# Gate's and up's products by kind in three pairs, Strassen-like sums rewritten, and a residual one step behind its chunk, in a hybrid Fourier and SSD block on one core

## The chip, the cores and the metric

The kernel runs on 1 core of one Trainium2 chip. The metric is the device time of one execution in microseconds (us). Before the change the median of 3 runs is 2445.47 us (2444.1 to 2446.0).

## The reference

One layer of a flow-matching generator over 2048 latent tokens of width 1024, with 256 context tokens as a prefix, all in fp32. Cut to what the change touches:

```python
def swiglu(h, w_gate, w_up, w_down):
    return (jax.nn.silu(h @ w_gate) * (h @ w_up)) @ w_down
...
        hx = modulate(rms_norm(x, g_pre_mix[l]), sm_x, cm_x)
        u_f, z, xs, Bm, Cm, dt_raw = mixer_inputs(hx, ...)
        y, _, _ = ssd_bidir(xs, Bm, Cm, dt_raw, ...)
        x = x + gm_x * rms_norm(mixer_output(u_f, z, xs, y, d_skip[l], g_ssd[l], w_out[l]), g_post_mix[l])

        hx2 = modulate(rms_norm(x, g_pre_ffn[l]), sf_x, cf_x)
        x = x + gf_x * rms_norm(swiglu(hx2, w_gate[l], w_up[l], w_down[l]), g_post_ffn[l])
```

The mixer is a projection of the normed input, a Fourier part of 256 channels, a bidirectional chunked scan of 12 heads of 64 channels (chunks of 128 tokens), and an output projection to 1024. `w_gate` and `w_up` are 1024 x 2816, `w_down` is 2816 x 1024.

## The kernel before, in words

**Precision.** Every fp32 matrix is split into two halves: `hi`, its value rounded to the format fp32r, and `lo`, what is left. A product is hi·hi + hi·lo + lo·hi, three matmuls. ACT writes the hi half (a cast), and DVE or POOL the lo half (a subtraction).

**Chunk steps.** Once the projections are done, `chunk_step` runs for the chunks c = 15 to 1 and `last_step` for chunk 0. A step makes a chunk's scan outputs (`outputs_mm`, the state's part `off`, and `offb`, to which POOL's product `xq` is added), its gate, its norm, and its output projection into PSUM (`out_mm`), and beside these it prepares the next chunk: `scores`, `weights` (ACT shifts and exponentiates the decays `ab` in place), `state_terms`, `skip_terms`. Three names stand for chunks in flight: `ch` is this step's, `pv` the one before, `ppv` the one before that. `fourier_out` copies ch's Fourier outputs from PSUM into `ch.o`. In the next step `mix_out(pv)` adds the scan's part to `pv.o`, and ACT sums its squares. One more step later `mix_scale(ppv)` scales `ppv.o` by the norm (DVE, 128x1024) and `residual(ppv, G)` adds it on POOL to `ppv.xr`, the input's rows, and stores the sum as `x2`. Both `o` and `xr` are tiles of the tag `raw` with four buffers, which the weights' loads use as well; `xr` is loaded by `residual_load(pv)`. In eight of the steps `tile_norm` and `tile_modulate` read 128 rows of `x2` again, norm them, transpose them on PE and write them, modulated, into `xf`: two tiles (tag A) that hold the 1024 tokens of the first pass of the MLP, as feature blocks.

**Gate and up.** `gate_up(p, blocks, step, last)` runs for two passes p of 1024 tokens. Each pass has NJ = 11 pairs j of two 128-wide column blocks. For gate (m = 0) and up (m = 1) of a pair, the 2x2 block product is made by a scheme with seven products i = 0 to 6 instead of eight. One product is 12 matmuls of 128x512: a block of weights `wa` against a block `slot` of the tokens.
- Token blocks: `Blocks` makes seven blocks of 128x2048 from `xf`, some of them sums or differences of others (`sum`), and writes hi and lo halves (`parts`) into slots of the tags q, B and C. In the trace the tag's name is the tile's: `slot`, `actB`, `actC`; `actA` is xf, and `t2` a temporary sum.
- Weight blocks: quarters of a pair's weights are loaded into `raw` on the SP queue. `weight_block` returns one of them or a sum, `ws` (POOL, 128x512, three buffers); `make` casts it and subtracts (ACT, DVE), two halves in `wa`.
- Products go into PSUM banks (`mm`, and `mbank`), and their sums are gathered in `u2`, `u3` and `sg`; gate's sums go through SiLU on ACT, and are multiplied by up's on DVE or POOL. `hidden` makes four sums `hs` of the activations and stores them for the down projection.

`sequence(p, j)` sets the order of the 14 products: gate's seven, then up's seven. Only the first pair of pass 0 has an order of its own, which mixes the two. `stream` lists all of them, and `next_w` makes the weights ahead of their products in that order.

**What sets the order.** Instructions on an engine run in the order written, as the generators in `steps(...)` are advanced. The part from the first pair of pass 0 on is written out by hand: `steps(run, n)` lets `gate_up` issue n products, and between them stand the pieces of `xs0` (sums and parts), the last chunks' `mix_out`, `mix_scale` and `residual`. In the remaining pairs of pass 0 `beside` advances `prepare`, which norms, transposes and modulates the tokens of pass 1 into `xf1`, and in the last pair `last0(i)` writes block i of pass 1 once up's product i of pass 0 is issued. In the kernel of the trace all computing is recorded by one helper, so all rows carry its line, L140, and are told apart by their tiles.

Of the kernel before, what the change touches and what calls it, by code (L numbers as in the profile page):

```python
# [12 lines left out]
F32 = mybir.dt.float32  # L13
# [148 lines left out]
def fourier_ssd_block(ctx, tc, a):  # L162
# [625 lines left out]
    def quad_load(j, m, h):  # L788
        if (j, m, h) not in quads and j < 2 * NJ:
            c = 256 * (j % NJ)  # L790
            quads[j, m, h] = wload(GATE_UP[m][:, 4 * h : 4 * h + 4, c : c + 256], [P, 4, 256])

    def quad(j, m, r, h):
        quad_load(j, m, h)
        return quads[j, m, h][:, :, r * P : (r + 1) * P]

    def weight_block(j, m, i):
        a11, a21 = (quad(j, m, r, 0) for r in range(2))
        key = j, m
        if i == 0:  # L800
            return a11
        if i in (1, 3) and key not in sums:
            s1, s2 = (ta[0].tile([P, 4, P], F32, tag="ws", name="ws", bufs=3) for _ in range(2))
            G.tensor_tensor(s1, a21, quad(j, m, 1, 1), op=ALU.add)
            G.tensor_tensor(s2, s1, a11, op=ALU.subtract)
            sums[key] = s1, s2
        if i in (1, 3):
            return sums[key][i == 1]
        if i in (4, 5):
            return quad(j, m, i - 4, 1)  # L810
        s = ta[0].tile([P, 4, P], F32, tag="ws", name="ws", bufs=3)
        if i == 2:
            G.tensor_tensor(s, a11, a21, op=ALU.subtract)
        else:
            G.tensor_tensor(s, quad(j, m, 0, 1), sums.pop(key)[1], op=ALU.subtract)
        return s
# [3 lines left out]
    def make(kind, p, j, m, i):  # L820
# [53 lines left out]
    def down_parts(p, i, f):  # L874
# [7 lines left out]
        def temp():  # L882
            return ta[0].tile([P, 512], F32, tag="ws", name="wt", bufs=3)
# [252 lines left out]
    def residual_load(ch):  # L1136
        if ch.c > 1:
            ch.xr = wp.tile([P, D], F32, tag="raw", name="xr", bufs=4) if ch.c > 2 else g_.tile([P, D], F32, tag="acc", name="xr")
        dma(ch.xr, x_d[ch.c * P : (ch.c + 1) * P, :])
# [33 lines left out]
    normed = {}  # L1173
# [21 lines left out]
    def chunk_step(c, ch, nx, pv, ppv):  # L1195
# [26 lines left out]
        norms()  # L1222
        steps(st, 1)
        steps(w, 1)
        steps(st, 1)
# [15 lines left out]
        if pv:  # L1241
            residual_load(pv)
# [7 lines left out]
        steps(md)  # L1250
        if c in TILE_AT:
# [5 lines left out]
    def last_step(ch, pv, ppv):  # L1257
# [6 lines left out]
        mix_scale(ppv)  # L1264
        residual(ppv, V)
        quad_load(0, 0, 1)
# [3 lines left out]
        r1 = group_norm(ch)  # L1270
        feed_forward(ch, pv)
        steps(r1)
        steps(r2)
# [52 lines left out]
    with tc.manual_schedule(engines=ordered):  # L1326
# [229 lines left out]
        ch, pv, ppv = pend[0], None, None  # L1556
# [4 lines left out]
        def feed_forward(ch, pv):  # L1561
# [4 lines left out]
            ff.x = xs0 = Blocks(xf, ta[0], "xt")  # L1566
            xs0.place(0, 0)
# [5 lines left out]
            hs["gmix"], pv.xr, ch.xr, ch.o = (rows[:, i] for i in range(4))  # L1573
            dma(hs["gmix"], mods_d[0].rearrange("a d -> (a d)").partition_broadcast(P))
            residual_load(pv)
            residual_load(ch)
            fourier_out(ch)
            fetch(2)
# [4 lines left out]
        turn = [0]  # L1583

        def slot(i=None):

            tag = "qBCBqqC"[turn[0] % 7 if i is None else i]
            turn[0] += i is None
# [4 lines left out]
        def mbank(tag="m"):  # L1593
            return ff.pac.tile([P, 512], F32, tag=tag, name="m" + tag, bufs=3 if tag == "m" else 1)

        def parts_into(sl, src, engine=V):
            S.copy(sl[:, 0], src)
            engine.tensor_tensor(sl[:, 1], src, sl[:, 0].bitcast(F32), op=ALU.subtract)

        class Blocks:  # L1600


            def __init__(self, xf, pool, tag):
                self.xf, self.pool, self.tag, self.slots = xf, pool, tag, {}

            def place(self, i, fixed=None):
                self.slots[i] = slot(fixed)

            def sum(self, i):
                x1, x2 = self.xf  # L1610
                if i == 3:
                    V.tensor_tensor(x1[:, 0:4], x2[:, 0:4], x1[:, 0:4], op=ALU.subtract)
                elif i == 1:
                    self.t2 = [self.pool.tile([P, 2, 512], F32, tag=self.tag, name="t2") for _ in range(2)]
                    for h in range(2):
                        V.tensor_tensor(self.t2[h], x2[:, 4 + 2 * h : 6 + 2 * h], x1[:, 2 * h : 2 * h + 2], op=ALU.subtract)
                elif i == 2:
                    V.tensor_tensor(x2[:, 0:4], x2[:, 4:8], x2[:, 0:4], op=ALU.subtract)
                else:
                    for h in range(2):  # L1620
                        x = x1[:, 4 + 2 * h : 6 + 2 * h]
                        G.tensor_tensor(x, x, self.t2[h], op=ALU.subtract)

            def parts(self, i, engine=V):
                x1, x2 = self.xf
                sl = self.slots[i]
                if i == 1:
                    for h in range(2):
                        S.copy(sl[:, 0, 2 * h : 2 * h + 2], self.t2[h])
                        engine.tensor_tensor(sl[:, 1, 2 * h : 2 * h + 2], self.t2[h], sl[:, 0, 2 * h : 2 * h + 2].bitcast(F32),  # L1630
                                             op=ALU.subtract)
                else:
                    src = {0: x1[:, 0:4], 2: x2[:, 0:4], 3: x1[:, 0:4], 4: x1[:, 4:8], 5: x1[:, 4:8], 6: x2[:, 4:8]}[i]
                    parts_into(sl, src, engine)

        def gate_up(p, blocks, step, last):

            late = idle
            for j in range(NJ):
                apart = p == 0 and j == 0  # L1640
                if apart:
                    b1 = [mm()[:, 0, :], mbank("t")]
                else:
                    bb = mm()
                    b1 = [bb[:, m, :] for m in range(2)]
                sg = None
                st = [SimpleNamespace() for _ in range(2)]
                for m, i in sequence(p, j):
                    s = st[m]
                    if i in (1, 2, 3):  # L1650
                        s.b = getattr(s, "b", {})
                        s.b[i] = mbank()
# [11 lines left out]
                    elif i == 1:  # L1664
                        V.tensor_tensor(s.u2, s.u2, ps, op=ALU.add)
                    elif i == 2:
                        s.u3 = ta[0].tile([P, 512], F32, tag="u", name="u3", bufs=4)
                        V.tensor_tensor(s.u3, s.u2, ps, op=ALU.add)
# [291 lines left out]
```

## Time and profile before

| | |
|---|---|
| median of 3 runs | 2445.47 us (2444.1 to 2446.0) |
| the profiled execution | 2440.59 us, of which the trace's span is 2438.8 us |
| PE, matmuls | 2284.8 us busy, 94% of the span |
| PE, weight loads (beside the matmuls) | 1866.6 us, 77% |
| DVE | 1677.3 us, 69% |
| ACT | 1113.0 us, 46% |
| POOL | 1094.6 us, 45% |
| DMA | 377.20 MB, 155 GB/s on average |

The shares are averages over stages that differ: projections, scan, chunk steps, gate and up, down. A matmul counts as busy until its modelled end, also where it is stretched or its input is late. The chunk steps lie at 732 to 1084 us of the span, the first pairs of pass 0 at 1084 to 1220, and the change from pass 0 to pass 1 at 1525 to 1590.

### The profile page before, as it was taken

The page shows a single profiled execution, that of the slowest core. Times are in us where ns is not written, and L with a number is a line of the kernel's source. Part 1 is how long each engine was busy: PE and PEld are TensorE (multiplying, and loading weights), DVE is VectorE, ACT ScalarE, POOL GpSimd, SP SyncE. Part 2 cuts the span into 40 slices and gives each one's busy share as a digit, 9 for nine tenths or more (in the row PEclk, how much of TensorE's full clock was granted, in tenths as well). Part 3 has the DMA queues.
Part 4 walks back from the last instruction along what each step waited for, and adds up shares of the span by engine and source line. Part 5 has one row for each costly group of instructions (what it writes and reads, how often), then busy time and mean ns, then how long its engine had stood idle before and what let it go on. Part 6 is the DMA issues. An engine that isn't in the chain of part 4 may idle for free. (4 is left out here: it accounts for less than half of the span.)

```text
span 2438.8 us, 30217 instructions
## 1 busy us (share of the span) xinstructions
PE 2284.8 (94%) x10861; PEld 1866.6 (77%) x10861; DVE 1677.3 (69%) x2241; ACT 1113.0 (46%) x2019; POOL 1094.6 (45%) x681
## 2 busy tenths in 40 slices
PE   7999798899989999977999999799999999998998
PEld 3887667777778888765788888588888888877886
DVE  3569878698977777777555555855555575779666
ACT  4435453354338677765533333333333335444444
POOL 2122627545552444435546556546555451525512
PEclk9999998999999999998999999999999999999999
DMA  9355436355476887733333233243233364547333
GB/s 309 125 156 163 142 101 201 123 176 159 153 250 211 250 248 238 233 129 117 102 118 109 95 100 99 95 156 108 95 108 102 106 220 160 170 142 277 101 123 117
DMA packets 272580, 377.20 MB, mean 155 GB/s; under 512 B 17111, under 2 KB 190115, under 8 KB 269358
## 3 DMA queue, kind: packets, MB, share of 16 engines
q1 hardware_dynamic: 243062, 344.49, 44.6%
q10 hardware_dynamic: 29368, 30.78, 3.7%
q8 instruction: 86, 1.41, 0.2%
q14 instruction: 64, 0.52, 0.1%
HBM read 280.49 MB, written 94.72 MB: 154 GB/s over the span
## 5 line engine op out<-in xcount | busy, mean ns | idle before, releaser
L140 PE MATMUL b<-wd,hd 128*128 128x512 f32 x1848 | 426.6, 392 | 12.7 <-DVE hd L140 10.1
L140 PEld LDWEIGHTS b<-wd,hd 128*128 128x128 f32 x1848 | 348.5, 189 | 90.6 <-DVE hd L140 13.1
L140 PE MATMUL mm<-slot,wa 128*128 128x512 f32 x1560 | 374.9, 393 | 12.6 <-ACT u L140 5.3
L140 PEld LDWEIGHTS mm<-slot,wa 128*128 128x128 f32 x1560 | 293.9, 189 | 76.3 <-ACT u L140 5.7
L140 DVE SCALAR_TENSOR_TENSOR acc<-u,convw,acc 128x992 f32<-128x992 f32 (+5 forms) x228 | 310.6, 1366 | 23.5 <-ACT acc L140 19.1
L140 PE MATMUL mm<-actB,wa 128*128 128x512 f32 x1056 | 259.7, 394 | 12.6 <-DVE wa L140 5.6
L140 PE MATMUL mm<-actC,wa 128*128 128x512 f32 x1056 | 258.4, 394 | 10.1 <-DVE sg L140 5.1
L140 PEld LDWEIGHTS mm<-actB,wa 128*128 128x128 f32 x1056 | 200.1, 190 | 56.5 <-DVE wa L140 6.4
L140 PEld LDWEIGHTS mm<-actC,wa 128*128 128x128 f32 x1056 | 200.4, 190 | 53.4 <-DVE sg L140 5.5
L140 ACT CAST wa<-ws 128x512 fp32r<-128x512 f32 x176 | 109.1, 622 | 270.8 <-PE mm L140 253.3
L140 PE MATMUL mm<-actA,hi 128*128 128x512 f32 x704 | 227.7, 404 | 3.8 <-DVE actA L140 2.7
L140 POOL TENSOR_TENSOR rq_y<-rq_ms,mhalf 128x1 f32<-128x1 f32 (+2 forms) x60 | 52.8, 886 | 325.9 <-DVE rq_ms L140 316.3
L140 DVE TENSOR_TENSOR wa<-ws,wa 128x512 fp32r<-128x512 f32 x176 | 153.3, 872 | 49.4 <-ACT wa L140 47.6
L140 POOL TENSOR_TENSOR ws<-raw 128x512 f32<-128x512 f32 x88 | 121.4, 1379 | 125.4 <-DVE wa L140 120.9
L140 DVE TENSOR_TENSOR u<-u,mm 128x512 f32<-128x512 f32 x132 | 90.6, 686 | 123.3 <-PE mm L140 123.1
L140 DVE TENSOR_TENSOR wa<-raw,wa 128x512 fp32r<-128x512 f32 x132 | 127.4, 966 | 49.0 <-ACT wa L140 48.6
L140 PEld LDWEIGHTS mm<-actA,hi 128*128 128x128 f32 x704 | 130.2, 191 | 33.3 <-issue 4.1
L140 POOL TENSOR_TENSOR adacc<-adacc,adaw 128x1024 f32<-128x1024 f32 x28 | 74.0, 2641 | 182.0 <-ACT adaw L140 178.4
L140 ACT CAST wa<-raw 128x512 fp32r<-128x512 f32 x132 | 82.2, 623 | 152.2 <-PE mm L140 148.0
L140 POOL TENSOR_TENSOR lo<-raw,hi 128x1024 fp32r<-128x1024 f32 x34 | 90.2, 2654 | 127.5 <-ACT hi L140 127.5
L140 PE MATMUL mm<-actC,hi 128*128 128x512 f32 (+1 forms) x512 | 144.7, 370 | 0.0
L140 PE MATMUL mm<-actA,lo 128*128 128x512 f32 x352 | 139.3, 396 | 0.6 <-DVE lo L140 0.6
(286 smaller groups left out, 4452.3 us busy)
## 6 DMA issues: line engine op xcount, KB each, us to landing
hraw<-hg SPq DMA_DIRECT2D x70, 512.0 KB, 4.5
raw<-in_w_in_dram SPq DMA_DIRECT2D x54, 512.0 KB, 4.9
ab<-acsd SPq DMA_DIRECT2D x128, 192.0 KB, 4.3
raw<-in_w_gate_dram SPq DMA_DIRECT2D x44, 512.0 KB, 5.0
raw<-in_w_up_dram SPq DMA_DIRECT2D x44, 512.0 KB, 5.2
hg<-hs SPq DMA_DIRECT2D x22, 1024.0 KB, 5.0
adaw<-in_w_ada_dram SPq DMA_DIRECT2D x32, 512.0 KB, 3.8
l_x<-xtok SPq DMA_DIRECT2D x33, 384.0 KB, 6.1
```

The costliest lines, as they stand in the source:

```text
L140: r = issue(out, *args, **kw)
```

## The change

It has two parts that meet at the first pair of pass 0.

**In the chunk steps** `ppv` goes. `mix_scale` and `residual` now take `pv`, the chunk of the step before, and stand later in the step, behind the first parts of the next chunk's weights and states; `residual_load(ch)` loads this step's own `xr`; `fourier_out` moves down behind `norms()`. In four of the steps, and after four pieces of `prepare`, `third_sum` makes a 128x4x128 piece of one block difference (b22 - b12), which `Blocks` made as a whole before. `last_step` and `feed_forward` follow.

**In gate and up** three pairs, `TOGETHER` (the first and the last of pass 0, the first of pass 1), take the products by kind: gate's 0, up's 0, gate's 4, up's 4, then 2, 1, 3, 6 and 5. In them the banks of products 1 and 3 are `m2` for gate and `t` for up, one buffer each; every bank tag now has one buffer. The two multiplications by up's sums that POOL made go to DVE there. `Blocks` is rewritten: each of the sums is made in place on DVE right before its block's halves, and all lo halves are DVE's; the slot's tag is fixed by the block's number. The quarters of the weights are loaded in the order of their first use by a list, `quarters`, the next whenever the one four places back has had its last use. `ws` has four buffers.

```diff
+    TOGETHER = ((0, 0), (0, NJ - 1), (1, 0))
+
     def sequence(p, j):
-        if p == 0 and j == 0:
-            return [(0, 0), (1, 0), (0, 4), (0, 1), (0, 2), (0, 3), (0, 6), (1, 4), (0, 5), (1, 1), (1, 2), (1, 3), (1, 5), (1, 6)]
+        if (p, j) in TOGETHER:
+            return [(m, i) for i in (0, 4, 2, 1, 3, 6, 5) for m in range(2)]
         return [(m, i) for m in range(2) for i in range(7)]
...
-        if i == 3:
-            jn, mn = (j, 1) if m == 0 else (j + 1, 0)
-            for h in range(2):
-                quad_load(jn, mn, h)
+        while len(quads) < len(quarters) and last_use[quarters[len(quads) - 4]] <= pos[1]:
+            quad_load()
...
+    def third_sum(xf, t):
+
+        if t > 3:
+            x = xf[1][:, :, (7 - t) * P : (8 - t) * P]
+            V.tensor_tensor(x[:, 0:4], x[:, 4:8], x[:, 0:4], op=ALU.subtract)
...
         steps(r2)
-        if ppv:
-            mix_scale(ppv)
-            residual(ppv, G if nx else V)
+        if third:
+            third_sum(xf, third.pop())
         fourier_mm(ch)
         steps(wo_rest.pop() if wo_rest else idle)
-        fourier_out(ch)
         steps(w, 1)
         steps(st, 2)
         steps(sk, 1)
         norms()
+        fourier_out(ch)
         steps(st, 1)
         steps(w, 1)
+        if pv:
+            mix_scale(pv)
+            residual(pv, G)
         steps(st, 1)
...
-        if pv:
-            residual_load(pv)
+        residual_load(ch)
...
-            xs0.place(4, 4)
-            xs0.parts(4, G)
+            steps(r1)
+            xs0.parts(4)
...
+            quad_load()
             fetch(2)
-            xs0.sum(3)
-            xs0.sum(1)
...
-            def parts(self, i, engine=V):
-                x1, x2 = self.xf
-                sl = self.slots[i]
+                b11, b21, b12, b22 = x1[:, 0:4], x1[:, 4:8], x2[:, 0:4], x2[:, 4:8]
                 if i == 1:
...
+                    V.tensor_tensor(b11, b11, b12, op=ALU.add)
+                elif i == 3:
+                    V.tensor_tensor(b12, b22, b11, op=ALU.subtract)
+                elif i == 5:
+                    V.tensor_tensor(b21, b21, b11, op=ALU.subtract)
+                src = {0: b11, 1: b11, 2: b12, 3: b12, 4: b21, 5: b21, 6: b22}[i]
+                sl = self.slots[i] = slot(i)
+                S.copy(sl[:, 0], src)
+                V.tensor_tensor(sl[:, 1], src, sl[:, 0].bitcast(F32), op=ALU.subtract)
...
-                        s.b[i] = mbank()
+                        s.b[i] = mbank(({1: "m2", 2: "m0", 3: "m2"}, {1: "t", 2: "m1", 3: "t"})[m][i] if together else f"m{i - 1}")
...
-                                (G if i != 6 else V).tensor_tensor(out, out, c, op=ALU.mult)
+                                (V if together or i == 6 else G).tensor_tensor(out, out, c, op=ALU.mult)
...
         def last0(i):
-            if i == 0:
...
-                xs1.parts(i, G if i in (3, 5) else V)
+            xs1.parts(i)
```

How this moves instructions shows at three places.

ACT in one of the chunk steps, from the scores to the square of the step before: `ab<-ab,lda` are the shifts of the decays, `ab<-ab` the exponentials, `o<-mm` is `fourier_out`. Before:

```order
L140 COPY sc<-a 128x512
L140 ACTIVATE off<-yg 128x768
L140 COPY o<-mm 128x1024
L140 ACTIVATE ab<-ab,lda 128x128 x12
L140 ACTIVATE ab<-ab 128x384
L140 ACTIVATE ab<-ab,lda 128x128 x6
L140 ACTIVATE ab<-ab 128x384
L140 ACTIVATE ab<-ab,lda 128x128 x6
L140 ACTIVATE ab<-ab 128x384 x2
L140 CAST yh<-off 128x256
L140 ACTIVATE jk,sq_6287<-o 128x1024
```

and now:

```order
L140 COPY sc<-a 128x512
L140 ACTIVATE off<-yg 128x768
L140 ACTIVATE ab<-ab,lda 128x128 x6
L140 COPY o<-mm 128x1024
L140 ACTIVATE ab<-ab,lda 128x128 x6
L140 ACTIVATE ab<-ab 128x384
L140 ACTIVATE ab<-ab,lda 128x128 x6
L140 ACTIVATE ab<-ab 128x384
L140 ACTIVATE ab<-ab,lda 128x128 x6
L140 ACTIVATE ab<-ab 128x384 x2
L140 CAST yh<-off 128x256
L140 ACTIVATE jk,sq_6292<-o 128x1024
```

The first six shifts stand ahead of the copy of o now, the other six still behind it.

PE in the first pair of pass 0, one row for a product: the bank it goes to, the token block (`slot`, `actB`, `actC`) and the weights. Before:

```order
L140 MATMUL mm_9166<-slot_9114,wa_9117 128x512 x12
L140 MATMUL mt_9167<-slot_9114,wa_9128 128x512 x12
L140 MATMUL mm_9166<-slot_9120,wa_9168 128x512 x12
L140 MATMUL mm_9242<-actB_9232,wa_9175 128x512 x12
L140 MATMUL mm_9266<-actC_9233,wa_9195 128x512 x12
L140 MATMUL mm_9294<-actB_9234,wa_9212 128x512 x12
L140 MATMUL mt_9167<-slot_9120,wa_9267 128x512 x12
L140 MATMUL mm_9413<-actB_9232,wa_9327 128x512 x2
L140 MATMUL mm_9294<-actC_9235,wa_9245 128x512 x12
```

and now:

```order
L140 MATMUL mm_9171<-slot_9127,wa_9130 128x512 x12
L140 MATMUL mm_9171<-slot_9127,wa_9146 128x512 x12
L140 MATMUL mm_9171<-slot_9137,wa_9172 128x512 x12
L140 MATMUL mm_9171<-slot_9137,wa_9175 128x512 x12
L140 MATMUL mm0_9260<-actB_9192,wa_9197 128x512 x12
L140 MATMUL mm1_9286<-actB_9192,wa_9220 128x512 x12
L140 MATMUL mm2_9306<-actB_9215,wa_9242 128x512 x12
L140 MATMUL mt_9332<-actB_9215,wa_9265 128x512 x12
L140 MATMUL mm2_9355<-actC_9283,wa_9287 128x512 x12
L140 MATMUL mt_9381<-actC_9283,wa_9307 128x512 x12
L140 MATMUL mm2_9355<-actC_9325,wa_9334 128x512 x12
L140 MATMUL mt_9381<-actC_9325,wa_9357 128x512 x12
```

Each token block is used by two products that follow each other, gate's and up's, where before several blocks were used by one product and again many places later; the banks `mm2` and `mt` come back after two products.

DVE in the last pair of pass 0, from the lo half of pass 1's block 0 (`slot`) on; 128x2048 is a block's lo half or a sum of blocks, `wa` the lo half of a weight block, `t2` half of a sum. Before:

```order
L140 TENSOR_TENSOR slot_12343<-actA_9321,slot_12343 128x2048
L140 TENSOR_TENSOR wa_12352<-raw_12190,wa_12352 128x512
L140 TENSOR_TENSOR actA_9321<-actA_9322,actA_9321 128x2048
L140 TENSOR_TENSOR u2_12341<-u2_12341,mm_12351 128x512
L140 TENSOR_TENSOR t2_12347<-actA_9322,actA_9321 128x1024
L140 TENSOR_TENSOR t2_12348<-actA_9322,actA_9321 128x1024
L140 TENSOR_TENSOR wa_12374<-raw_12190,wa_12374 128x512
L140 TENSOR_TENSOR actB_12368<-t2_12347,actB_12368 128x1024
L140 TENSOR_TENSOR u3_12389<-u2_12341,mm_12373 128x512
L140 TENSOR_TENSOR actA_9322<-actA_9322 128x2048
L140 TENSOR_TENSOR actB_12368<-t2_12348,actB_12368 128x1024
L140 TENSOR_TENSOR wa_12398<-ws_12396,wa_12398 128x512
```

and now:

```order
L140 TENSOR_TENSOR slot_12199<-actA_9379,slot_12199 128x2048
L140 TENSOR_TENSOR wa_12204<-ws_12202,wa_12204 128x512
L140 TENSOR_TENSOR wa_12226<-ws_12223,wa_12226 128x512
L140 TENSOR_TENSOR actA_9379<-actA_9379,actA_9380 128x2048
L140 TENSOR_TENSOR sg_12219<-sg_12219,mm_12162 128x512
L140 TENSOR_TENSOR slot_12244<-actA_9379,slot_12244 128x2048
L140 TENSOR_TENSOR wa_12252<-ws_12249,wa_12252 128x512
L140 TENSOR_TENSOR wa_12273<-ws_12222,wa_12273 128x512
L140 TENSOR_TENSOR actA_9379<-actA_9379 128x2048
L140 TENSOR_TENSOR actB_12288<-actA_9380,actB_12288 128x2048
L140 TENSOR_TENSOR wa_12292<-ws_12248,wa_12292 128x512
L140 TENSOR_TENSOR u2_12178<-u2_12178,mm2_12291 128x512
```

The sums stand each right before the halves of their block, with nothing in temporaries, and between them stand the weights of the pair's remaining products; the lo halves of two blocks that were POOL's are in this queue.

## Rows read from the trace of the kernel before

**Rows 1.** The page, its first line

```profile
span 2438.8 us, 30217 instructions
```

**Rows 2.** Busy time by stretch: PE, weight loads, DVE, ACT, POOL, clock, DMA

```profile
732.00:1084.00 352.00, 333.77 (x2010) 282.70 (x2009) 269.23 (x543) 260.17 (x655) 144.79 (x111) 1.00 0.72 222
1084.00:1220.00 136.00, 107.31 (x459) 83.46 (x458) 91.23 (x95) 70.64 (x137) 72.92 (x51) 0.92 0.35 111
...
1525.00:1590.00 65.00, 49.94 (x195) 38.50 (x195) 56.98 (x41) 26.92 (x32) 36.97 (x17) 0.92 0.34 104
```

**Rows 3.** PE's waits in 1084 to 1220, then 1525 to 1590: us, times, longest

```profile
PE mm L140 <- ACT u L140: 5.3, 1, 5.3
PE mm L140 <- DVE sg L140: 5.1, 1, 5.1
...
PE mm L140 <- DVE u L140: 8.1, 3, 5.1
PE mm L140 <- DVE wa L140: 7.0, 4, 4.7
```

**Rows 4.** PE in order of time: start, us, then operation and count

```profile
1084.03 0.61 PE L140 MATMUL mm<-slot,wa 128*128 128x512 f32 x2
...
1215.20 2.88 PE L140 MATMUL mm<-actB,wa 128*128 128x512 f32 x12
1217.92 3.33 PE L140 MATMUL mm<-slot,wa 128*128 128x512 f32 x14
```

**Rows 5.** DVE in order of time, from pass to pass

```profile
1538.27 0.68 DVE L140 TENSOR_TENSOR wa<-raw,wa 128x512 fp32r<-128x512 f32 x1
1538.87 2.28 DVE L140 TENSOR_TENSOR actA<-actA 128x2048 f32<-128x2048 f32 x1
...
1546.28 6.33 DVE L140 TENSOR_TENSOR actA<-actA 128x2048 f32<-128x2048 f32 x1
```

**Rows 6.** POOL beside it, and groups of POOL and DVE in 1220 to 1500

```profile
1545.86 4.60 POOL L140 TENSOR_TENSOR actB<-actA,actB 128x2048 fp32r<-128x2048 f32 x1 [11.52 <-ACT actB L140]
...
L140 POOL TENSOR_TENSOR ws<-raw,ws 128x512 f32<-128x512 f32 x15 | 19.3, 1290 | 45.0 <-DVE wa L140 45.0
...
L140 DVE TENSOR_TENSOR sg<-sg,u 128x512 f32<-128x512 f32 x8 | 14.2, 1772 | 0.0
```

**Rows 7.** Groups of ACT in 1525 to 1590: the cast of a block

```profile
L140 ACT CAST slot<-actA 128x2048 fp32r<-128x2048 f32 x3 | 5.7, 1907 | 4.7 <-POOL actA L140 4.7
```

**Rows 8.** Waits of PE and of ACT in the chunk steps

```profile
PE y L140 <- DVE offb L140: 8.6, 8, 1.5
PE a L140 <- DVE off L140: 4.5, 5, 1.2
...
ACT o L140 <- POOL xr L140: 41.0, 8, 5.2
```

**Rows 9.** One chunk step in order of time: DVE, POOL, ACT, PE; offb's addition

```profile
989.88 1.27 DVE L140 SCALAR_TENSOR_TENSOR o<-o,rq_y,gmix 128x1024 f32<-128x1024 f32 x1
...
991.53 2.36 POOL L140 TENSOR_TENSOR xr<-xr,o 128x1024 f32<-128x1024 f32 x1
994.29 1.82 POOL L140 TENSOR_TENSOR xq<-l_x,dq 128x768 f32<-128x768 f32 x1 [0.40 <-DVE dq L140]
...
993.92 1.02 ACT L140 COPY o<-mm 128x1024 f32<-128x1024 f32 x1 [5.12 <-POOL xr L140]
...
1004.31 0.87 PE L140 MATMUL y<-ident,offb 128*128 128x128 f32 x6 [1.02 <-DVE offb L140]
...
L140 DVE TENSOR_TENSOR offb<-offb,xq x16: 941/946/959, 745.6 to 1068.0; 128x768 f32<-128x768 f32 x16
```

**Rows 10.** The page, DMA issues: queue, count, KB each, us to landing

```profile
raw<-in_w_gate_dram SPq DMA_DIRECT2D x44, 512.0 KB, 5.0
```

**Rows 11.** DVE at the end of the last step

```profile
1077.73 1.22 DVE L140 TENSOR_TENSOR xr<-xr,o 128x1024 f32<-128x1024 f32 x1
...
1078.87 2.28 DVE L140 TENSOR_TENSOR slot<-actA,slot 128x2048 fp32r<-128x2048 f32 x1
```

More of the change, by code (lines that the diff above doesn't have):

```diff
@@ L786, in fourier_ssd_block, with quad_load @@
     pos = [0, 0]
[L788 to L791, printed above, removed]
+    quarters, last_use = [], {}
+    for n, (kind, p, j, m, i) in enumerate(stream):
+        if kind == "a":
+            for h in {0: (0,), 1: (0, 1), 2: (0,), 3: ()}.get(i, (1,)):
+                if (j + NJ * p, m, h) not in last_use:
+                    quarters.append((j + NJ * p, m, h))
+                last_use[j + NJ * p, m, h] = n
+    def quad_load():
+        j, m, h = quarters[len(quads)]
+        c = 256 * (j % NJ)
+        quads[j, m, h] = wload(GATE_UP[m][:, 4 * h : 4 * h + 4, c : c + 256], [P, 4, 256])
     def quad(j, m, r, h):
-        quad_load(j, m, h)
         return quads[j, m, h][:, :, r * P : (r + 1) * P]
     def weight_block(j, m, i):
-        a11, a21 = (quad(j, m, r, 0) for r in range(2))
         key = j, m
         if i == 0:
[L801 to L805, printed above, removed]
+            return quad(j, m, 0, 0)
+        if i in (4, 5):
+            return quad(j, m, i - 4, 1)
+        if i == 1:
+            s1, s2 = (ta[0].tile([P, 4, P], F32, tag="ws", name="ws", bufs=4) for _ in range(2))
+            G.tensor_tensor(s1, quad(j, m, 1, 0), quad(j, m, 1, 1), op=ALU.add)
+            G.tensor_tensor(s2, s1, quad(j, m, 0, 0), op=ALU.subtract)
             sums[key] = s1, s2
@@ L1263, in last_step @@
         square_sums(ch)
-        mix_scale(ppv)
-        residual(ppv, V)
-        quad_load(0, 0, 1)
+        steps(r2)
+        mix_scale(pv)
+        residual(pv, V)
+        if third:
+            third_sum(xf, third.pop())
+        quad_load()
         fourier_mm(ch)
@@ L1269, in last_step @@
         out_mm(ch.py, ch, range(2, KD), 0)
[L1270 to L1273, printed above, removed]
+        feed_forward(ch, group_norm(ch))
         out_mm(ch.py, ch, range(2, KD), 1)
@@ L1639, in gate_up @@
             for j in range(NJ):
[L1640 to L1645, printed above, removed]
+                together = (p, j) in TOGETHER
+                if together:
+                    step(99)
+                bb = mm()
+                b1 = [bb[:, m, :] for m in range(2)]
                 sg = None
-                st = [SimpleNamespace() for _ in range(2)]
+                st = [SimpleNamespace(b={}) for _ in range(2)]
                 for m, i in sequence(p, j):
@@ L1663, in gate_up @@
                         S.copy(s.u2, ps)
[L1664 to L1668, printed above, removed]
+                    elif i in (1, 2):
+                        if i == 1:
+                            V.tensor_tensor(s.u2, s.u2, ps, op=ALU.add)
+                        if 1 in s.b and 2 in s.b:
+                            s.u3 = ta[0].tile([P, 512], F32, tag="u", name="u3", bufs=4)
+                            V.tensor_tensor(s.u3, s.u2, s.b[2], op=ALU.add)
                     else:
@@ L1731, in prepare, with beside @@
                 yield
+                third_sum(xf1, t)
         pre = [idle]
[L1735 to L1736 removed]
+        def beside(n=2):
+            steps(pre[0], n)
         def last0(i):
[L1739 to L1749 removed]
+            xs1.parts(i)
         def last1(i):
```

125 lines of the change are left out of this document (42 added, 83 removed).

## The prediction, made before the changed kernel ran

> **What bounds the kernel now.** The page comes first: the span is 2438.8 us [rows 1], and the matrix engine (PE) is busy for most of it, so a change can only bring what PE now waits. The table of stretches says where that is [rows 2]: in 732 to 1084 (the chunk steps, with the last step), in 1084 to 1220 (the first pairs of gate and up) and in 1525 to 1590 (from the first pass to the second). The reader is to see PE's busy time fall behind the stretch there, and PE's granted clock at 0.92 in the last two, a mixture of its levels of 2.4 GHz (1.00) and 1.2.
>
> A product is 12 matmuls; two that follow each other undisturbed start 2.72 us apart [rows 4], 0.227 us for a matmul. From this the losses come out. In 1084 to 1220 stand 459 instructions, of them 64 transposes with a quarter of the columns: 395 x 0.227 + 64 x 0.057 = 93 us of work in 136, so 43 us are lost (**stretch A**). In 1525 to 1590, 195 x 0.227 = 44 of 65: 21 us (**stretch B**). In both, the waits of PE name ACT and DVE results: a block not ready (u, sg, wa) [rows 3]. In the chunk steps PE's waits are 8.6 us for offb in 8 steps and 4.5 us for off in 5 [rows 8]: 13 us (**stretch C**). Behind offb stands ACT: in the same number of steps, 8, it waited for POOL's xr before it copied o, 41.0 us in all [rows 8], since o wants a buffer that the residual two steps back still held. One such step: xr runs from 991.53, ACT's copy waits 5.12 us for it, the decay shifts follow, and at its end PE waits 1.02 us for offb [rows 9].
>
> **The change part by part, from one execution.** The profiled one took 2440.6 us (span 2438.8), 4.9 below the median 2445.5 of the runs; the sum is made against 2440.6 and the 4.9 is added again.
>
> *C, the residual one step behind.* The buffer that o takes is now free before the step, and the first six shifts stand ahead of the copy. ACT's 41 us of waits go, and the shifts start some 5 us earlier in 8 steps. What follows on DVE (select, offb, the sum of squares) comes earlier, and PE's 13 us with it. Against that: the scaling of o (1.27 us) stands behind the first select, so xr (2.36) and xq (1.82) [rows 9] follow later on POOL, and offb needs xq; and four steps get a subtraction of 512 columns, 0.68 each [rows 5], hidden while ACT is late. On the SP queue the store of xr waits longer, and the loads behind it with it; those of ab wait for PE anyway. Bounds: 13 saved, or 1 us lost in each of 15 steps. I take 9 of the 13: the cover is thinner but holds. The load of weights costs nothing: four quarters of 5.0 us [rows 10], three of them asked for before the last step, the fourth once o of chunk 1 is free, near 1080; product (1,4) wants it near 1092.
>
> *A, the first pair.* Before, each block fed one product after the first; now it feeds two, 5.44 us. The lo halves and sums that POOL made (4.6 for a half [rows 6]) are DVE's now, 2.28 each [rows 5]. Count DVE's work up to the lo half of block 5, the last: 7 halves and 3 sums at 2.28 are 22.8; 14 weight halves and 9 additions or multiplications at 0.68 are 15.6; two scalings at 1.27, one addition at 1.22 [rows 9, 11], a norm and four small ones make 5: 43.5 us. It starts where block 0's half now starts, 1078.87, right behind the residual's addition [rows 11], later by a subtraction of 0.68 and by the wait for the root of that residual, near 1 us since the square runs beside DVE's sums: 1080.5. Behind this wait stand block 0's half and the first weights; PE is at the mixer's last outputs until 1084.03. Waits in the queue: behind the first two sums ACT's cast, 1.9 each [rows 7]; the square of the last mixer output, near 2; and xn of the next pass, whose root stands on POOL behind four weight sums, near 4 (1.29 each [rows 6]). With some 2 us of POOL's instructions in between, block 5 is ready near 1135 to 1136. Without loss its product would start at 1084.03 + 12 x 2.72 = 1116.7 [rows 4]; so the pair loses about 20. Behind it the 64 transposes stay as they are, and I leave them the 9 us that they and the clock lose now. A loses 29 instead of 43: **14 saved**. Bounds: DVE without any wait, 7 + 9 = 16 lost, 27 saved; or as late as now, nothing saved. Between them I lie near the middle, since the waits come from the written order.
>
> *B, from pass to pass.* Block i of pass 1 can be written once pair 10's second product has used block i of pass 0, and is wanted 12 products (32 us) later; before it was 16. DVE's work from block 0's half to the weights of pass 1's first product: 11 weight halves, 9 others at 0.68, 4 halves and 3 sums at 2.28, 29.6 us. It can begin 7.3 us after the pair's start (two products and a cast) and is wanted at 38.1: it just fits, 30.8. What decides is POOL, which has some 8 sums of 1.29 in that time. The rows show what happens when both want memory: a sum that takes 2.28 took 6.33 beside a POOL half of 4.60, and a product of two tiles in memory 1.77 instead of 0.68 [rows 5, 6]. So the instructions add rather than overlap: 29.6 + 10.3 = 40, 9 us late, and a bank (m2 or t, one buffer each) that DVE reads late holds up the product two places on. With 3 us more in the next pair B loses 12 of its 21: **9 saved**. Bounds: all of the POOL work falls into DVE's gaps, 2 lost, 19 saved; or 21 as now.
>
> The Trainium skill ("SBUF — State Buffer", section "SBUF: two separate sides") has it that VectorE with two operands in SBUF and GpSimd take one port pair by an exclusive lock for a whole instruction. It speaks against moving work to DVE while POOL keeps its sums. The 6.33 agrees with it; without it B would lose 2, the bound above.
>
> The two multiplications that go from POOL to DVE in each of three pairs are in the counts; the fourth buffer for ws costs memory alone.
>
> **Sum:** 9 + 14 + 9 = 32 us. 2440.6 - 32 = 2408.6 for a profiled execution, 2413.5 for the median. Its own range, with half the distance to the bounds of A and B and 4 us either way for C, is 2398 to 2429.
>
> **The rivals.**
> 1. *DVE has room.* POOL fits the gaps and the chain of A has no waits: 27 + 19 + 11, 57 saved, 2388. For it: DVE is busy 57 of 65 and 91 of 136 us [rows 2] with stretched instructions. Against it: each sum is followed at once by a half that needs ACT's cast.
> 2. *DVE becomes the bound.* In the three pairs the queue runs as late as POOL's halves do now, because POOL's sums, held to four ws buffers, in turn wait for DVE: A and B save 3 together, C 9: 12 saved, 2433. For it: 40 us of work for 31 in B. Against it: POOL loses halves of 4.6 to 5 us.
> 3. *Slower: the late xr.* In each chunk step offb needs xq, behind xr, behind the scaling: 1.27 + 2.36 + 1.82 = 5.45 us, then 0.95 for the addition [rows 9]. PE took offb at 1004.31, so the scaling must start by 997.9; it started at 989.88 [rows 9], so it may slip 8.0 us. Behind offb's first half and the first select it would slip 7.4 if ACT came no earlier: the point is within reach. Past it each step pays the excess, with the store and the loads behind it some 2 us: 15 x 2 = 30 lost in C, against 23 saved in A and B: 2452. Against it: ACT's 5.12 us are freed by the same edit.
> 4. *Nothing seen:* the same chain pays 1.5 us a step and eats what A and B bring, 2445.
>
> **How the numbers follow.** Forecast 0.54; rival 1 0.13; rival 2 0.19; rival 3 0.08; rival 4 0.06. About 0.2% (4.9 us) is what a measurement can tell from no change. Forecast, rival 1 and nearly all of rival 2 are faster: 0.85; rival 4 and the edge of rival 2 within: 0.07; rival 3: 0.08. The range 2392 to 2437 takes in the forecast's bounds and rival 2, and leaves out rival 3, rival 4 and most of rival 1.
>
> **What would show it.** C: ACT's wait for xr before o gone, PE's wait for offb under 3 us in all. A: waits of PE in products 8 to 12 of the pair, for u, sg and the last block, none before; the loss up to the first pair's end near 20. B: about 12 lost, named by DVE, u before wa; DVE's halves at 2.3 to 3.6, no POOL half left. Wrong would be: PE waiting longer for offb than now; DVE idle while PE waits in B (then it is not DVE's work); a granted clock below 0.92 in A or B, since PE's waits would then be longer than now.

## The result and the profile after

The changed kernel takes 2410.86 us (median of 4 runs, 2409.39 to 2411.72), the kernel before on the same chip 2444.78 (4 runs, 2440.51 to 2446.0): a ratio of 0.9865, 95% interval 0.9852 to 0.9879, so about 34 us faster. The forecast was 2413.5 in 2392 to 2437. Against the profiled execution of before, the span fell from 2438.8 to 2407.6, by 31.2 where the sum had said 32. From the page of the changed kernel, its span and the busy time of each engine (PEld are the weight loads):

```profile
span 2407.6 us, 30176 instructions
...
PE 2281.4 (95%) x10861; PEld 1865.9 (77%) x10861; DVE 1669.3 (69%) x2255; ACT 1113.6 (46%) x2017; POOL 1049.4 (44%) x667
```

PE does the same work, 10861 matmuls. POOL lost 45 us of busy time, most of it the lo halves, sums and multiplications that DVE makes now. DVE is busy 8 us less all the same (1677.3 before): the 22 multiplications `sg<-sg,u` that it made before took 1.77 us each, the 28 of now 0.80 on average.

Where the 31.2 came from is read from landmarks that both kernels have: PE's first product of gate and up; ACT's copy of u, which follows the first product of gate and of up in every pair; and the end of the span. Pairs are counted on through both passes, so pair 11 is the first of pass 1. ACT's row for pair 3 and for pair 12, of the kernel before:

```profile
1248.04 0.59 ACT L140 COPY u<-mm 128x512 f32<-128x512 f32 x1 [2.09 <-PE mm L140]
...
1611.78 0.59 ACT L140 COPY u<-mm 128x512 f32<-128x512 f32 x1 [2.10 <-PE mm L140]
```

and of the changed one:

```profile
1220.85 0.59 ACT L140 COPY u<-mm 128x512 f32<-128x512 f32 x1 [2.10 <-PE mm L140]
...
1574.57 0.59 ACT L140 COPY u<-mm 128x512 f32<-128x512 f32 x1 [2.04 <-PE mm L140]
```

| landmark | before | after | shift | part | forecast |
|---|---|---|---|---|---|
| first product of gate and up | 1084.03 | 1068.97 | -15.1 | C, chunk steps: 15.1 saved | 9 |
| u of pair 3 | 1248.04 | 1220.85 | -27.2 | A, first pairs: 12.1 saved | 14 |
| u of pair 12 | 1611.78 | 1574.57 | -37.2 | B, pass to pass: 10.0 saved | 9 |
| end of the span | 2438.8 | 2407.6 | -31.2 | the down stage: **6.0 given back** | 0 |

From pair 3 to pair 10, and from pair 12 to the end of pass 1, the shift stays the same to 0.01 us: outside the three stretches nothing moved. In the down stage, whose own code the change leaves as it was, 3.5 us are lost at its start and the rest in small steps.

In the chunk steps the waits of PE that [rows 8] show are nearly gone. PE's waits of the changed kernel there (us, times, longest):

```profile
PE y L140 <- DVE offb L140: 1.3, 8, 0.2
...
PE a L140 <- DVE off L140: 0.8, 1, 0.8
```

Before, a third one stood beside the two of [rows 8], in the same view of the kernel before:

```profile
PE a L140 <- POOL rq_y L140: 2.9, 10, 0.4
```

ACT has no wait for xr left at all. A wait of 1.2 us of PE for `dg` is new; it stands in the first step alone, and is 0.2 at most in the other executions with these chunk steps. In the first pair PE looks like this, one row for each product or run of products (the view of [rows 4]):

```profile
1068.97 2.88 PE L140 MATMUL mm<-slot,wa 128*128 128x512 f32 x12
1072.84 3.03 PE L140 MATMUL mm<-slot,wa 128*128 128x512 f32 x12 [0.99 <-ACT u L140]
1076.55 3.02 PE L140 MATMUL mm<-slot,wa 128*128 128x512 f32 x12 [0.68 <-ACT u L140]
1086.16 5.05 PE L140 MATMUL mm<-slot,wa 128*128 128x512 f32 x12 [6.59 <-ACT sg L140]
1091.04 8.36 PE L140 MATMUL mm<-actB,wa 128*128 128x512 f32 x36
1099.24 2.88 PE L140 MATMUL mt<-actB,wa 128*128 128x512 f32 x12
1104.07 4.58 PE L140 MATMUL mm<-actC,wa 128*128 128x512 f32 x12 [1.95 <-DVE u L140]
1112.71 5.38 PE L140 MATMUL mt<-actC,wa 128*128 128x512 f32 x12 [4.05 <-DVE u L140]
```

The waits at products 9 and 10 were expected. Those at products 2 to 4, 8.3 us together, were not: these products wait for ACT's reads of the product before, although up's products go to another half of the tile than gate's.

### The profile page after: what moved, and what is told of

Same layout as the page of the kernel before. It is cut to its first block, busy times and chain, and to the rows that moved or that the text cites. A ratio compares the mean times of both kernels' runs of the same rounds, so it can differ in the third digit from the quotient of the medians.

```text
span 2407.6 us, 30176 instructions
## 1 busy us (share of the span) xinstructions
PE 2281.4 (95%) x10861; PEld 1865.9 (77%) x10861; DVE 1669.3 (69%) x2255; ACT 1113.6 (46%) x2017; POOL 1049.4 (44%) x667
## 5 line engine op out<-in xcount | busy, mean ns | idle before, releaser
L140 POOL TENSOR_TENSOR ws<-raw 128x512 f32<-128x512 f32 x88 | 127.4, 1448 | 310.3 <-DMA raw<-in_w_up_dram 131.4
L140 PE MATMUL mm<-actC,wa 128*128 128x512 f32 x984 | 241.5, 394 | 7.4 <-DVE u L140 7.2
L140 PE MATMUL mm<-actB,wa 128*128 128x512 f32 x1020 | 239.4, 390 | 0.0
L140 PEld LDWEIGHTS mm<-actC,wa 128*128 128x128 f32 x984 | 186.6, 190 | 47.6 <-issue 8.7
L140 PEld LDWEIGHTS mm<-actB,wa 128*128 128x128 f32 x1020 | 191.2, 188 | 39.6
L140 POOL TENSOR_TENSOR rq_y<-rq_ms,mhalf 128x1 f32<-128x1 f32 (+2 forms) x60 | 43.1, 723 | 288.6 <-DVE rq_ms L140 274.5
L140 DVE TENSOR_TENSOR wa<-raw,wa 128x512 fp32r<-128x512 f32 x132 | 118.4, 898 | 65.2 <-ACT wa L140 64.7
```

What stands on the lines that cost most here:

```text
L140: r = issue(out, *args, **kw)
```

## The experiments

Chunk steps start at 753 to 758 us in these executions, so shifts are taken between landmarks of one run. Runs of one kernel lie up to 7 us apart (the kernel before: 2439.57 to 2446.97 on all chips used), so what a single run shows is read from its trace.

### 1. The banks of the first four products

```diff
-                b1 = [bb[:, m, :] for m in range(2)]
+                b1 = [bb[:, 0, :], mbank("t") if together else bb[:, 1, :]]
```

> In the three pairs up's products 0 and 4 go to the bank t instead of the other half of gate's tile. Theory (one PSUM tile for both is what PE waits for): the waits of PE for ACT's copy of u and for ACT's sg in the first pair (0.99, 0.68 and 6.59 us) go, the first pair ends 5 to 8 us earlier, pair 2 starts at a shift of -33 us or more against the kernel before instead of -27.2, and the time is near 2404 us. Rival (DVE's queue is what binds the pair): the same microseconds come back at up's product 2 or at the next products as waits for wa or u, and the time stays within 2 us of 2411.

Measured: 2404.11 us (ratio to before 0.9836, 0.982 to 0.9851). PE's rows:

```profile
1071.60 2.88 PE L140 MATMUL mm<-slot,wa 128*128 128x512 f32 x12
1074.32 2.88 PE L140 MATMUL mt<-slot,wa 128*128 128x512 f32 x12
1077.04 2.88 PE L140 MATMUL mm<-slot,wa 128*128 128x512 f32 x12
1079.76 2.88 PE L140 MATMUL mt<-slot,wa 128*128 128x512 f32 x12
...
1086.89 0.73 PE L140 MATMUL mm<-actB,wa 128*128 128x512 f32 x2 [1.53 <-ACT wa L140]
1089.30 6.91 PE L140 MATMUL mm<-actB,wa 128*128 128x512 f32 x22 [1.68 <-DVE wa L140]
...
1103.91 4.44 PE L140 MATMUL mm<-actC,wa 128*128 128x512 f32 x12 [4.99 <-DVE u L140]
1112.54 5.18 PE L140 MATMUL mt<-actC,wa 128*128 128x512 f32 x12 [4.19 <-DVE u L140]
```

The three waits are gone, so they came from one tile for both: the program orders a write to one half behind a read of the other. But from the first product to u of pair 1 it takes 65.4 us instead of 67.9: of the 8.3 us only 2.5 stay saved, the rest comes back at product 6, which waits twice (1.53 and 1.68), and at 9 and 10, 9.2 us together instead of 6.0. So in the first pair most of it went as the rival said: DVE's and ACT's queues bind it. From pass to pass 2.3 us more are saved, and the down stage gives back 1.3 us less. The time agrees with the theory's 2404 by the sum of these places, not by the first pair; the shift of -33 that was expected at pair 2 did not come.

### 2. The tags of blocks 2 and 3

```diff
-            tag = "qBBCqqC"[i]
+            tag = "qBCBqqC"[i]
```

> The token blocks 2 and 3 swap the tags of their slots (C and B, as in the kernel before). Theory (the down stage gives back 6 us, of which 3.5 at its start, because the load of a down weight into tag C waits for block 3 and so one product longer): that load is issued 2.7 us earlier against the last pair, PE's wait for ACT's hd (1.65 us) at the start of the down stage goes, the shift there stays at -37 instead of falling to -33.8, and the time is 2407 to 2409. Rival (the loss is the phase of other DMA): no change, 2411.

Measured: 2405.54 us (0.9843, 0.9827 to 0.986). This interval and the changed kernel's overlap, so the reading rests on the traces. SP's issue of the down weight to tag C, and POOL's sum that waits for it, in the changed kernel:

```profile
1944.48 0.37 SPq L868 DMA_DIRECT2D actC<-in_w_down_dram  x1
```

```profile
1952.41 2.99 POOL L140 TENSOR_TENSOR actA<-actC,actA 128x512 f32<-128x512 f32 x2 [5.42 <-DMA actC<-in_w_down_dram]
```

and with the tags back:

```profile
1942.10 0.37 SPq L868 DMA_DIRECT2D actC<-in_w_down_dram  x1
```

```profile
1950.09 2.99 POOL L140 TENSOR_TENSOR actA<-actC,actA 128x512 f32<-128x512 f32 x2 [2.77 <-DMA actC<-in_w_down_dram]
```

The last pair runs 0.33 us later here, so the load is 2.7 us earlier, one product. POOL's wait falls by as much, and the sums hs behind it are earlier. ACT's cast hd came right behind these sums in the changed kernel, and PE waited for it at the start of the down stage:

```profile
PE b L140 <- ACT hd L140: 1.7, 1, 1.7
```

With the tags back this wait is gone, and the shift against before stays at -36.9 over the start of the down stage. At the last landmark it is -35.7 where the changed kernel had -31.2. So most of the six microseconds were the price of a letter: with block 3 in tag C instead of block 2, that buffer is used one product longer, and the first load into it waits for that.

### 3 and 4. The chunk steps: a free buffer, or the order on ACT

Experiment 3 puts ACT's copy back to its old place and leaves the residual one step behind; experiment 4 takes the kernel before, residual two steps behind, and moves only the copy.

```diff
         steps(wo_rest.pop() if wo_rest else idle)
+        fourier_out(ch)
         steps(w, 1)
...
         norms()
-        fourier_out(ch)
         steps(st, 1)
```

> ACT's copy of o stands where it stood before, ahead of all shifts; the residual stays one step behind. Theory (a free buffer is what brought the 15 us of the chunk steps): ACT has no wait for xr, steps with a tile stay near 20.3 us, the first product of gate and up starts at 1069 to 1071. Rival (the six shifts ahead of the copy brought it): the copy now waits for the Fourier outputs of PE with the shifts behind it, steps with a tile go back to 22 to 23 us, and the first product starts near 1080.

```diff
         steps(wo_rest.pop() if wo_rest else idle)
-        fourier_out(ch)
         steps(w, 1)
...
         norms()
+        fourier_out(ch)
         steps(st, 1)
```

> The kernel before with one edit: ACT's copy of o behind the norms and the first parts of the weights, the residual two steps behind as it was. Theory (the free buffer): ACT still waits for POOL's xr, less than 41 us in all since the copy comes later; at most a third of the 15 us is gained, the first product starts at 1079 to 1084. Rival (the order on ACT): steps with a tile take near 20.3 us and the first product starts at 1069 to 1072.

Measured from the starts of PE's `y<-ident,offb` in steps 5 to 13, by pattern (two steps with a tile of the first pass's tokens, one without):

| kernel | steps with a tile | without | first product of gate and up | the same, from the first step on | time |
|---|---|---|---|---|---|
| before | 23.1 and 22.1 | 19.5 | 1084.03 | 330.6 | |
| changed | 20.2 and 20.2 | 19.5 | 1068.97 | 315.4 | 2410.86 |
| 3: copy back, residual one behind | 20.3 and 20.2 | 19.5 | 1068.98 | 314.0 | 2407.55 (one run) |
| 4: copy late, residual two behind | 20.8 and 20.3 | 19.0 | 1067.44 | 312.5 | 2424.53 (one run) |

Each alone brings all of it: from the first step on the changed kernel is 15.2 us shorter than before, experiment 3 16.6 and experiment 4 18.1. The theory of the free buffer holds in experiment 3, and falls in 4, whose first product of gate and up comes even before the 1069 to 1072 of the rival: there ACT still waits, but the wait is filled. ACT's rows of one such step in experiment 4:

```profile
978.30 1.85 ACT L140 ACTIVATE ab<-ab,lda 128x128 f32<-128x128 f32 x6
983.52 1.02 ACT L140 COPY o<-mm 128x1024 f32<-128x1024 f32 x1 [3.37 <-POOL xr L140]
```

and the waits of ACT and of PE in its chunk steps (us, times, longest):

```profile
ACT o L140 <- POOL xr L140: 22.8, 8, 3.4
```

```profile
PE y L140 <- DVE offb L140: 1.1, 1, 1.1
```

The wait for xr falls from 5.12 us [rows 9] to 3.37, by about the 1.85 of the six shifts that stand ahead of it now. PE's wait for offb, 8.6 us in eight steps before, is one of 1.1: in the steps PE had waited at most 1.5 us for it, less than the six shifts take. One moved line in the kernel before gives 17 to 18 us, half of the whole change. The residual one step behind adds nothing to it, and its price shows in the steps without a tile, 19.5 instead of 19.0, where PE waits up to 0.2 us for offb.

### 5 and 6. From pass to pass: POOL's sums, and two products for a block

Experiment 5 leaves out POOL's weight sums in the two pairs; experiment 6 takes the products by kind in the first pair only.

```diff
+        if j in (NJ - 1, NJ):
+            return quad(j, m, 0, 0 if i == 2 else 1)
         if i == 1:
```

> The changed kernel, but in the last pair of the first pass and the first of the second POOL makes no weight sums: the products take a loaded quarter in their place, so those products compute other numbers. From pass to pass (from the copy of u of pair 10 to that of pair 12, 76.2 us without loss) the changed kernel takes 87.2, 11 lost. Theory (POOL's sums stretch DVE's instructions, 2.28 to 3.4, and hold it up): the loss falls to 4 to 6 us. Rival (the loss stands between ACT's casts, DVE's order and the banks): it stays at 9 to 11.

```diff
-    TOGETHER = ((0, 0), (0, NJ - 1), (1, 0))
+    TOGETHER = ((0, 0),)
```

> Only the first pair takes its products by kind; the last pair of the first pass and the first of the second take gate's seven and then up's, with the rewritten sums on DVE. Theory (two products for a block are what hides the blocks' making): the loss from pass to pass goes from 11 us back to 18 to 22, time 2418 to 2422. Rival (the sums and halves taken from POOL are what brought it): the loss stays at 10 to 13, time within 2 us of 2411.

From the copy of u of pair 10 to that of pair 12, 76.2 us without loss:

| kernel | us | lost |
|---|---|---|
| before | 97.2 | 21.0 |
| changed | 87.2 | 11.0 |
| 5: no weight sums (2403.14, one run) | 83.2 | 7.0 |
| 6: by kind only in the first pair (2415.05, one run) | 91.3 | 15.1 |

DVE's sums and halves in the changed kernel's last pair of pass 0, and a sum of POOL beside one:

```profile
1497.00 3.38 DVE L140 TENSOR_TENSOR actA<-actA 128x2048 f32<-128x2048 f32 x1
...
1504.82 3.38 DVE L140 TENSOR_TENSOR actA<-actA 128x2048 f32<-128x2048 f32 x1
1508.13 3.36 DVE L140 TENSOR_TENSOR actB<-actA,actB 128x2048 fp32r<-128x2048 f32 x1
```

```profile
1498.20 3.35 POOL L140 TENSOR_TENSOR ws<-raw,ws 128x512 f32<-128x512 f32 x1
```

and the first and the last of these three in experiment 5:

```profile
1496.65 2.29 DVE L140 TENSOR_TENSOR actA<-actA 128x2048 f32<-128x2048 f32 x1
...
1505.80 2.29 DVE L140 TENSOR_TENSOR actB<-actA,actB 128x2048 fp32r<-128x2048 f32 x1
```

All ten such instructions of the last pair take 2.28 to 2.29 there; in the changed kernel four of the ten take 3.36 to 3.38 and a fifth 2.79. 3.36 to 3.38 is about what one of 2.28 and one of POOL's 1.29 [rows 6] take behind each other (3.57). The Trainium skill ("SBUF — State Buffer", section "SBUF: two separate sides") states that DVE and POOL share a port pair under an exclusive lock, held for a whole instruction. The trace agrees, and shows the wait inside both instructions' durations, 3.38 and 3.35, not as idle time before them. PE's wait for u in this stretch falls with it, changed kernel first:

```profile
PE mm L140 <- DVE u L140: 5.2, 1, 5.2
```

```profile
PE mm L140 <- DVE u L140: 2.2, 1, 2.2
```

So POOL's sums cost 4.0 of the 11 us, not the 9 that the sum had given them, and a loss of 7.0 is above the 4 to 6 that the theory expected. Experiment 6 lies between its two expectations: of the 10.0 us saved from pass to pass, 4.1 are due to the order by kind with what hangs on it in the code (the banks, two multiplications on DVE). The other 5.9 belong to the rest of the change, the rewritten sums, the halves moved from POOL to DVE, the order of the loads and the fourth `ws` buffer, which no run tells apart.

### 7, 8 and 10. The order of DVE's queue in the first pair

In the changed kernel DVE's queue ahead of the addition that frees bank t (`u<-u,mt`) is this:

```profile
1108.12 0.15 DVE L140 TENSOR_SCALAR rq_ms<-sq 128x1 f32<-128x1 f32 x1 [1.15 <-ACT actA L140]
1110.61 0.75 DVE L140 TENSOR_SCALAR xn<-xn,rq_y 128x1024 f32<-128x1024 f32 x1 [2.34 <-POOL rq_y L140]
1111.28 0.68 DVE L140 TENSOR_TENSOR wa<-ws,wa 128x512 fp32r<-128x512 f32 x1
1111.88 0.68 DVE L140 TENSOR_TENSOR u<-u,mt 128x512 f32<-128x512 f32 x1
```

That instructions run in the order written holds only inside the code's `manual_schedule` block, which ends with `xs0.parts(5)`. The norms of the second pass (xn) stand behind it; the program's scheduler fitted them in between. Experiment 7 extends the hand-written part to the end of the third pair, experiment 8 adds the edits of 1 and 2.

```diff
-    xf1 = [act("A", F32) for _ in range(2)]
...
-    pre[0] = prepare()
+        steps(run, 5)
+        xf1 = [act("A", F32) for _ in range(2)]
...
+        pre[0] = prepare()
+        steps(run, 28)
     steps(run, 999)
```

> The changed kernel with the first norms for the second pass put behind the first pair's last product (the hand-written order reaches to the end of the third pair). Theory (in the first pair DVE's queue binds, and in it xn, which waits 1.15 us for ACT's square and 2.34 us for a root that stands behind two weight sums on POOL, holds up the addition that frees bank t): PE's wait of 4.05 us at up's product 3 goes, from the first product to the third pair the time falls by 4 to 5 us, the whole to 2406. Rival (the chain of casts on ACT and halves on DVE binds, with or without it): less than 1.5 us, 2410 to 2411.

> Three edits together: up's products 0 and 4 in bank t, the tags of blocks 2 and 3 swapped back, and the norms of the second pass behind the first pair. If they act in different places (2.5 us in the first pair and 2.3 from pass to pass by the first, 4.9 in the down stage by the second, 4 in the first pair by the third) the sum is 13 to 14 us against the changed kernel: 2397. If the first and the third compete for one chain of DVE in the first pair: 2400 to 2402.

Measured: 2460.37 us (1.0073, 1.0057 to 1.009) and 2447.95 (1.0022, 1.0009 to 1.0035; runs from 2442.2 to 2454.8). The expected times missed in both. In experiment 7 PE's wait at product 10 is still there without xn ahead of it, and DVE, ahead of the addition that ends it, now waits for ACT's cast of a weight block:

```profile
1109.73 4.58 PE L140 MATMUL mt<-actC,wa 128*128 128x512 f32 x12 [4.25 <-DVE u L140]
```

```profile
1107.90 1.09 DVE L140 TENSOR_TENSOR wa<-ws,wa 128x512 fp32r<-128x512 f32 x1 [2.54 <-ACT wa L140]
```

ACT in turn had waited 4.40 us for POOL's sum of that block, which stands behind a root on POOL. So xn alone did not hold product 10 up: it starts 42.8 us after the first instead of 43.7, within the 1.5 us of the rival, and product 12 at 56.8 instead of 52.1. By the copy of u of pair 3 some 50 us are lost, most of them in the two pairs behind the first, which the written order now covers too: transposes stand there ahead of products and are not ready. PE's waits of experiment 7 in these two pairs, 29 us, with the granted clock at 0.83 in 1137 to 1271:

```profile
PE mt L140 <- ACT actA L140: 15.5, 8, 2.8
PE mt L140 <- DVE xn L140: 13.8, 7, 6.1
```

Experiment 10 keeps the scheduler's part as it is, takes the edits of 1 and 2, and moves the last chunk's output sum behind up's product 1. ACT's scratch tile gets another tag for it.

```diff
-        steps(run, 1)
-        r2 = mix_out(pv, ta[0], "u")
-        steps(run, 1)
+        steps(run, 2)
         xs0.parts(6)
-        steps(r2)
-        steps(run, 1)
-        mix_scale(pv)
-        residual(pv, V)
         steps(run, 1)
+        r2 = mix_out(pv, ta[0], "sg")
+        steps(run, 1)
+        steps(r2)
+        mix_scale(pv)
+        residual(pv, V)
         xs0.parts(5)
```

> The two edits, and the last chunk's output sum (with ACT's square of it) moved from ahead of block 6 to behind up's product 1, in the first pair. Theory (the order of DVE's and ACT's queues binds products 9 and 10: ACT waits 3.6 us for that sum while a cast and block 6 stand behind it, and the norms of the second pass move behind it too): the waits of PE at products 9 and 10 (4.99 and 4.19 us with the banks apart) fall to 4 or less together, from the first product to the end of the first pair 4 to 6 us less, the whole 2394 to 2398. Rival (it is the amount of DVE's work in the pair, whatever its order): the waits move to products 11 to 14, the whole as without it within 2 us.

Measured: 2405.1 us (0.9846, 0.9832 to 0.9859), 5 more than the two edits alone: neither expectation of the time came. PE's rows at products 9, 10 and 13, and in the next pair:

```profile
1100.28 3.00 PE L140 MATMUL mm<-actB,wa 128*128 128x512 f32 x12 [2.38 <-DVE u L140]
1105.54 4.57 PE L140 MATMUL mt<-actB,wa 128*128 128x512 f32 x12 [2.26 <-DVE u L140]
...
1120.10 2.93 PE L140 MATMUL mm<-slot,wa 128*128 128x512 f32 x6 [2.84 <-DVE wa L140]
...
1149.96 0.30 PE L140 MATMUL mt<-ident,xn 128*128 128x128 f32 x1 [4.63 <-DVE xn L140]
```

The two waits are 4.6 us together, near the 4 that the theory said (8.2 with the two edits alone), and product 13 starts 46.1 us after the first instead of 52.3. But two matmuls on PE waits 2.84 us for the weights' half that DVE makes later now: product 14 starts at 54.8, against 55.6. In pair 1, where xn is late too, the rest and 1.8 us more are lost by its seventh product. (Of the 5 us another 3.0 stand at the first chunk step already, ahead of every edit; whether they are this kernel's or this execution's stays open.) So the waits moved to products 11 to 14, as the rival said, and on into the next pair: what DVE puts off in the first pair is missed soon after.

### 9. The edits of experiments 1 and 2 together

> The first two edits alone: up's products 0 and 4 in bank t, and the tags of blocks 2 and 3 swapped back. They act in different stretches (4.8 us in the first pair and from pass to pass; 4.9 in the down stage): 2399 to 2402. If the down stage's loss were only moved, 2404.

Measured: the edits of experiments 1 and 2 together take 2399.98 us (0.9826, 0.9812 to 0.9839), as expected. That is 11 us less than the changed kernel by the medians, which come from different chips, and 9.6 by the spans of the traces. The two act in different stretches and nearly add up: alone they brought 6.8 and 5.3 by the medians. It is the fastest of all that ran.

## Why the prediction was right, and where its terms were off

The time and its sign were right, the cause mostly. That the total of 32 comes so near to 31.2 is luck in part: two errors of 6 us, in C and in the down stage, have opposite signs.

- **C: 9 taken of at most 13; measured 15.1.** The term was mis-sized by its bound. The 13 was the sum of PE's waits for offb and off [rows 8]; PE also waited 2.9 us for a root on POOL, which I had not counted, and with it the list of before reaches 16. The price of the chain on the other side (later xr) was right in kind: 0.5 us in a step without a tile. What this part of the prediction named as its two causes, the free buffer and the six shifts ahead of the copy, are alternatives: experiments 3 and 4 show either to be enough. PE's wait for offb is 1.3 us, under the 3 that was asked for.
- **A, 14; measured 12.1.** DVE's work was counted about right: from block 0's half (1065.39) to the end of block 5's (1124.9) it took 59.5 us, where 55 had been counted; product 13 starts 54.9 us after the first, 22 later than without loss, where about 20 had been said. The places of the waits were half right: products 9 and 10 for u, as said, but "none before" was wrong, for the shared tile costs 8.3 us at products 2 to 4. That these waits add only 2.5 us to the pair (experiment 1) says that DVE's queue was behind them, as argued, with ACT's casts and POOL's sums in its chain (experiment 7).
- **B, 9; measured 10.0, loss 11.0 against 12 said.** PE waits 5.2 us for DVE, for u and not for wa, at product 9, where m2 comes back after two products; DVE's halves take 2.3 to 3.4. The working was right in mechanism and wrong in size: POOL's sums were to make all of the 9 us, and make 4.0 (experiment 5). The other 7 us are there without them; about 2.3 of them are the shared tile's (experiment 1), the rest no run takes apart.
- **The down stage, put at nothing; measured 6.0 given back.** No term of the sum and no rival had it. The new fixed tags were read for where blocks of a pass come free for the next, not for who takes the buffer at the very end of pass 1 (experiment 2).
- **Rivals and signs.** "DVE has room" (2388) did not come: A still loses about 31 us and B 11. "DVE becomes the bound" (2433) is partly what A shows, yet without eating the gain. "Slower: the late xr" and "nothing seen" did not come: offb is late by 0.2 us at most, since ACT, free of its wait for xr, came earlier, as the objection had it. Of the three signs of being wrong none came: PE waits less for offb, DVE works all through PE's 5.2 us in B, and the granted clock is 0.94 in 1069 to 1220 and 0.96 in 1487 to 1575.

## What to carry to other kernels

When an in-order engine waits for a buffer, look first whether ready work stands behind the waiting instruction: moving one copy behind six shifts brought as much as making the buffer free a step earlier. When buffers get new names or tags, follow each to its last reader in the program, there too where the next stage loads into it. Two halves of one tile are one thing to the program's dependencies, and a write to one waits for a read of the other: give them tiles of their own where a reader is late.

## What the runs showed of the hardware

Behind these waits of PE its granted clock was lower, so that more was lost than the wait alone. Stretches of the changed kernel around its wait of 6.59 us (columns as in [rows 2]):

```profile
1082.00:1086.00 4.00, 0.00 (x0) 0.00 (x0) 2.29 (x2) 3.97 (x4) 0.87 (x1) 0.72 0.05 15
1086.00:1090.00 4.00, 3.84 (x9) 3.07 (x10) 1.29 (x3) 0.61 (x2) 1.73 (x1) 0.50 0.09 8
```

and of experiment 1, where PE works in the first of these and has its waits of 1.53 and 1.68 us in the second:

```profile
1082.00:1086.00 4.00, 3.36 (x15) 2.44 (x13) 2.38 (x2) 1.59 (x1) 3.28 (x1) 1.00 0.45 131
1086.00:1090.00 4.00, 1.43 (x5) 0.92 (x6) 3.62 (x4) 3.22 (x5) 0.61 (x1) 1.00 0.00 0
1090.00:1094.00 4.00, 4.00 (x13) 3.08 (x12) 2.77 (x3) 0.62 (x1) 1.11 (x1) 0.58 0.31 58
```

In the changed kernel the granted clock is 0.50, the level of 1.2 GHz, right after the idle stretch, and the product that starts there takes 5.05 us instead of 2.88. In experiment 1 it is 1.00 in both stretches, 2.4 GHz, and falls behind its own waits, to 0.58 in the next. The instructions of DVE and POOL that hold each other up, 3.36 to 3.38 us where 2.28 is usual, stand above.
